# Moving the operand splits around the output projection of a neighbourhood-attention layer, and one more up product ahead of the second half

## The chip, the cores and the metric

The kernel runs on one core of one Trainium2 chip. The metric is the device time of one execution in microseconds; the time given for a kernel is the median of several runs.

## The reference

One trunk of two layers over 1024 latent tokens (a grid 64 wide) and 256 context tokens, width 1024. Layer 0 mixes with grouped-query attention and a bidirectional recurrence; layer 1, which the change touches, mixes with 2-D neighbourhood attention over 16 heads of 64 channels, then projects the heads' outputs with `w_out` (1024 x 1024). Both layers end with a gated feed-forward net of 2816 channels with a width-3 convolution. Cut to layer 1:

```python
h = rms_norm(x, norm_pre_mix) * (1 + sc1) + sh1
y = neighbourhood_attention(h, h_ctx) @ odd_w_out            # (1024, 1024)
x = x + g1 * rms_norm(y, norm_post_mix)
h = rms_norm(x, norm_pre_ffn) * (1 + sc2) + sh2
a, g = split(conv3(h @ w_up) + b)
x = x + g2 * rms_norm((silu(g) * a) @ w_down, norm_post_ffn)
```

## The kernel before

Every product is done at nearly float32 accuracy on TensorE by splitting each operand into a rounded part and a remainder and adding three products: rounded x rounded, rounded x remainder, remainder x rounded. A **split** is two instructions: ScalarE (ACT) writes the rounded part with a cast, then another engine subtracts it from the raw tile to get the remainder. In `w_split` the raw tile is a piece of `w_out` (`w_raw`, 128x512, two buffers), the parts are `w_hi` and `w_lo`; in `o_split` it is a 128-channel chunk of the attention's output (`o_raw`, one buffer; read back from the scratch `ocd`), the parts are `o_h` and `o_l`. Remainders of both are subtracted on VectorE (DVE).

**Attention** (`odd_attention`) runs 128 jobs, one for each of 8 tiles of 128 queries of 16 heads. The Python loop makes one pass per job, called a *turn* here, and six more passes that finish the last jobs (the *drain*). The order in which the passes write instructions is the order on PE, ACT, DVE and POOL (`in_order`). A turn holds: the scores `c_s` of job i (PE); their maximum, the *reduce*, with the bias (DVE, `c_p<-c_s`); the exponential of job i-1 (ACT); the transposes `c_pt` of job i-3 (PE) and the split of what they give (`c_ph` on ACT, `c_pl` on DVE); half of the value products `c_pv` of an earlier pair (PE); the reciprocal `rl` of job i-1 (DVE) and the *divide* by it (POOL, `c_p<-c_p,rl`); every second turn `finish` (ACT `c_o`, DVE), whose results go to `ocd`, or for the last two heads to the tile `oL`.

Between these, `step(n)` draws n pieces from the generator `fill`. It first gives the projections of q and k, and when they are used up, shortly before turn 112, it gives `odd_out_ahead`: the splits of `w_out`'s first half (columns 0 to 511), of the chunks of `o`, the first k-steps of the output projection (`out_step`, tiles 0 and 1, columns 0 to 511, three matmuls each) and then the splits of `w_out`'s second half, in the order they are written there, some 2.5 pieces in a turn, so that they lie between other instructions of a turn.

**Output projection and norm** (`odd_out_norm`): after the drain, `steps()` writes 114 k-steps (three matmuls each) into four PSUM banks, and between them the work on finished tiles (square, root, scaling, residual: `square`, `post`, `add`, `squares`, `scale`). The tile's bank is used again by a later tile, so a k-step can wait for `post` (DVE, `y<-g_ps`). The second half of the tokens needs its own `o_split` of each chunk, read from `ocd` again; they are written at steps 2, 4, ... 16.

**Feed-forward front** (`second_front`): first products of the up projection run before the second half of the tokens is normalised. `first(j)` is a product of the weight quarter `A11` of channel block j, `first_out(j)` copies its result out of PSUM (`f_p`), and a second product with the quarter `A12` adds to the same bank. `second_half` then transposes the second half of the tokens (`n_pc`, `n_pt`, `n_pv`), and splits the sums that a Strassen-like scheme needs. `split` here leaves its remainder to GpSimd (POOL).

Of the kernel before, what the change touches and what calls it, by code (L numbers as in the profile page):

```python
# [11 lines left out]
F32 = mybir.dt.float32  # L12
# [3 lines left out]
OP = mybir.AluOpType  # L16
# [4 lines left out]
P = 128  # L21
# [44 lines left out]
class Trunk:  # L66
# [1227 lines left out]
    def odd_out_norm(self, xs, first_half, op, load, early):  # L1294
# [66 lines left out]
        def steps():  # L1361
            seq = [(0, 0, KT - 1), (1, 0, KT - 1)]
            seq += [(i, 1, k) for i in range(2) for k in range(KT)]
            seq += [(i, h, k) for i in range(2, 8) for h in range(2) for k in range(KT)]
            chains, waits, groups = [], [], list(range(KT))
            for n, (i, h, k) in enumerate(seq):
                if (i, h) not in ps:
                    ps[i, h] = self.banks2[2 * h + i if i < 2 else 2 * (i % 2) + h]
                self.out_step(i, h, k, ps[i, h])
                for f in waits:  # L1370
                    f()
                waits = []
                for c in list(chains):
                    if next(c, "end") == "end":
                        chains.remove(c)
                if k == KT - 1:
                    if h == 0:
                        ms1[i] = self.small.tile([P, 2], F32, name="y_ms")
                        waits.append(lambda i=i: square(ps[i, 0], ms1[i], 0))
                    elif i < 7:  # L1380
                        chains.append(chain(i))
                if n % 2 == 0 and 2 <= n < 2 + 2 * KT:
                    c = (n - 2) // 2
                    self.o_split(raws[c] if c < KT - 1 else self.oL, c, 1)
# [12 lines left out]
            for c in chains:  # L1397
                for _ in c:
                    pass
# [21 lines left out]
    def ffn_up(self, l, src, ctx, x_src, x_dst, hp, pp, tp, es, beside):  # L1421
# [123 lines left out]
        def second_front():  # L1545
# [24 lines left out]
            pp, tp = (self.pool(es, n, 1, space=PSUM) for n in ("u_psum", "t_psum"))  # L1570
            first(0)
            first_out(0, self.wp.tile([P, 512], F32, name="f_p1", tag="w_A21h", bufs=1))
            next(tail)
            product(st["G", 0][:, :512], ("A12",), "B21", False, True)
            split(1, "A11")
            first(1)
            for _ in tail:
                pass
            nx.close()
            sp, cw = up_pool()  # L1580
            total(0, "S1", "A21", OP.add, "A22")
# [7 lines left out]
            next(sums)  # L1589
            return sp, cw, sums  # L1590

        X, sp = {}, None
        with self.in_order(*self.compute, behind=l == 1), ExitStack() as loads:
            sp, cw, sums = second_front() if l == 1 else up_front()

# [1 line left out]
            for j in range(FK):  # L1597
# [8 lines left out]
                if j:  # L1606
                    gate_start(j - 1)
                    split(j, "S4")
                if j or l == 0:
                    product(st["G", j][:, :512], ("A12",), "B21", False, True)  # L1610
                if j:
                    gate_end(j - 1)
# [550 lines left out]
    def odd_attention(self, gp, tp, pp, sp):  # L2163
# [197 lines left out]
        at = {"job": 0}  # L2361
        fill = project()

        def step(n):
            for _ in range(n):
                next(fill, None)

        jobs = [(h, b, ql) for h in range(CH) for b in (0, 3, 1, 2) for ql in range(2)]
        with self.in_order(*self.compute):
# [52 lines left out]
    def odd_out_ahead(self, at):  # L2422


        nc, a = self.nc, self.a
        W, O, raws = self.oW, self.oX, {}
        halves = [(k, h) for h in range(2) for k in range(KT)]

        def w_load(m):
# [5 lines left out]
        def w_split(m):  # L2435
# [3 lines left out]
            hi, lo = (w[:, 512 * h:512 * h + 512] for w in W[k])  # L2439
            raw = raws.pop(m)  # L2440
            nc.scalar.copy(hi, raw)
            nc.vector.tensor_tensor(out=lo, in0=raw, in1=hi.bitcast(F32), op=OP.subtract)
            w_load(m + 2)

        def o_load(c):
# [2 lines left out]

        w_load(0)
        w_load(1)  # L2450
        for m in range(2):
            w_split(m)
            yield
        while at["job"] < 112:
            yield
        o_load(0)
        w_split(2)
        yield
        for k in range(6):
            if k + 3 < KT:  # L2460
                w_split(k + 3)
                yield
            self.o_split(raws["o"], k, 0)
            if k < 5:
                o_load(k + 1)
            yield
            for i in range(2):
                self.out_step(i, 0, k, self.banks2[i])
                yield
        for m in range(KT, 2 * KT):  # L2470
            w_split(m)
            if m == KT + 3:
                o_load(6)
            yield
        self.o_split(raws["o"], 6, 0)
        yield
        for i in range(2):
            self.out_step(i, 0, 6, self.banks2[i])
            yield

    def o_split(self, raw, k, half):

# [210 lines left out]
```

## Time and profile before

| | us |
|---|---|
| median of 3 runs (3399.95 to 3403.27) | 3402.81 |
| profiled execution, whole | 3395.78 |
| its span | 3393.9 |
| layer 1, last turns and drain (2535 to 2608 of the span) | 73 |
| output projection and norm (2608.5 to 2698.1) | 89.6 |
| feed-forward front and block 0 (2698 to 2757) | 59 |

Times in the profile are microseconds from the span's start. A timeline row gives start, duration, engine, source line, operation and, in brackets, how long the engine was idle before it and what ended that. A windows row gives, for a stretch, its length, then busy time and number of instructions of PE, PEld (weight load), DVE, ACT and POOL, the granted TensorE clock (1.00 is full), the busy share of the DMA engines and GB/s.

### The profile page before, as it was taken

How to read it: one execution, taken by the hardware profiler on the slowest of the kernel's cores; microseconds unless marked ns; L12 is line 12 of the kernel's file. 1: busy time of each engine (PE TensorE's matmuls, PEld its weight loads, DVE VectorE, ACT ScalarE, POOL GpSimd, SP SyncE). 2: the span in 40 equal slices, each digit the busy share in tenths (PEclk: the TensorE clock that was granted, in tenths of full speed). 3: DMA queues.
4: the chain of work that ended last, by engine and by line, in shares of the span. 5: the costliest groups of instructions: out<-in, count | busy, mean ns of one | idle time of the engine just before them, and what ended most of it. 6: DMA issues, size and time to landing. Idle time of an engine off the chain costs nothing.

```text
span 3393.9 us, 48741 instructions
## 1 busy us (share of the span) xinstructions
PE 3117.6 (92%) x18364; PEld 2565.9 (76%) x18364; DVE 2038.5 (60%) x3421; ACT 1485.7 (44%) x2643; POOL 1528.8 (45%) x1155
## 2 busy tenths in 40 slices
PE   5899998869999599999999989999997989999997
PEld 2776776658887488888878768889986758888785
DVE  3625666647775754454577773377776465555778
ACT  3223222256664543333434353466665443433443
POOL 1310111187775466666620011577763367777201
PEclk8999999969999699999999989999999989999998
DMA  7524333321111221111275773222224212222856
GB/s 235 161 94 137 126 122 119 102 89 38 51 44 55 104 73 69 67 69 68 73 269 182 273 247 124 75 67 62 65 71 145 101 63 81 85 84 76 279 184 211
DMA packets 201100, 393.48 MB, mean 116 GB/s; under 512 B 23184, under 2 KB 84624, under 8 KB 200864
## 3 DMA queue, kind: packets, MB, share of 16 engines
q1 hardware_dynamic: 191680, 358.38, 32.2%
q0 software_dynamic: 9184, 31.99, 2.5%
q8 instruction: 144, 2.36, 0.3%
q14 instruction: 92, 0.75, 0.1%
HBM read 316.86 MB, written 73.81 MB: 115 GB/s over the span
## 4 chain that ended last, share of the span: by engine, by line
PE 76%; DVE 10%; DMA 4%; ACT 4%; issue 3%; POOL 2%; SPq 1%; POOLq 0%; ACTq 0%; DVEq 0%
PE g_ps L119 21%; PE u_g L119 13%; PE d_ps L119 11%; PE u_v L119 10%; PE u_pc L119 4%; PE a_pv L119 2%; PE c_pv L119 2%; PE c_s L119 2%; PE a_pt L949 2%; PE c_pt L2325 2%; PE mod_ps L119 1%; DVE a_pl L951 1%; PE a_s L119 1%; PE o_ps L119 1%; ACT a_ph L950 1%
## 5 line engine op out<-in xcount | busy, mean ns | idle before, releaser
L127 POOL TENSOR_TENSOR rs_r<-rs_e,mhalf 128x1 f32<-128x1 f32 (+3 forms) x106 | 81.5, 769 | 965.7 <-DVE rs_e L126 965.6
L119 PE MATMUL d_ps<-d_Bh,d_Ah 128*128 128x512 f32 x704 | 276.8, 393 | 10.6 <-ACT d_Bh L1739 10.3
L2308 POOL TENSOR_SCALAR c_p<-c_p,rl 128x640 f32<-128x640 f32 (+1 forms) x128 | 231.7, 1811 | 111.9 <-DVE rl L2307 86.4
L119 PE MATMUL d_ps<-d_Bl,d_Ah 128*128 128x512 f32 x704 | 277.8, 395 | 3.1 <-DVE d_Bl L1740 2.7
L119 PE MATMUL d_ps<-d_Bh,d_Al 128*128 128x512 f32 x704 | 276.5, 393 | 2.0 <-DVE d_Al L1740 1.9
L929 POOL TENSOR_SCALAR a_p<-a_p,rl 128x1280 f32<-128x1280 f32 (+1 forms) x80 | 240.0, 3002 | 72.4 <-DVE rl L928 60.4
L119 PE MATMUL g_ps<-xh,w_hi 128*128 128x512 f32 (+1 forms) x640 | 257.3, 402 | 7.9 <-ACT w_hi L563 6.5
L119 PE MATMUL g_ps<-xh,w_lo 128*128 128x512 f32 (+1 forms) x640 | 238.2, 372 | 2.6 <-POOL w_lo L2208 1.4
L119 PE MATMUL g_ps<-xl,w_hi 128*128 128x512 f32 (+1 forms) x640 | 238.7, 373 | 0.0
L1461 DVE TENSOR_TENSOR f_u<-u_v,f_p 128x512 f32<-128x512 f32 x88 | 60.5, 688 | 186.1 <-PE u_v L119 186.1
L951 DVE TENSOR_TENSOR a_pl<-a_pt,a_ph 128x512 fp32r<-128x512 f32 (+1 forms) x200 | 118.8, 603 | 85.0 <-ACT a_ph L950 84.9
L119 PEld LDWEIGHTS d_ps<-d_Bh,d_Ah 128*128 128x128 f32 x704 | 133.4, 189 | 40.7 <-ACT d_Bh L1739 11.4
L1447 POOL TENSOR_TENSOR w_S4l<-w_s,w_S4h 128x512 fp32r<-128x512 f32 x44 | 57.1, 1298 | 231.0 <-ACT w_S4h L1446 231.0
L119 PEld LDWEIGHTS d_ps<-d_Bl,d_Ah 128*128 128x128 f32 x704 | 133.2, 189 | 35.3 <-DVE d_Bl L1740 6.2
L119 PEld LDWEIGHTS g_ps<-xh,w_hi 128*128 128x128 f32 x640 | 122.3, 191 | 47.0 <-issue 27.5
L119 PEld LDWEIGHTS d_ps<-d_Bh,d_Al 128*128 128x128 f32 x704 | 133.5, 190 | 30.6 <-DVE d_Al L1740 3.3
L950 ACT CAST a_ph<-a_pt 128x512 fp32r<-128x512 f32 (+1 forms) x200 | 102.8, 518 | 121.0 <-PE a_pt L949 120.9
L2328 DVE TENSOR_TENSOR c_pl<-c_pt,c_ph 128x256 fp32r<-128x256 f32 (+1 forms) x256 | 113.7, 470 | 53.4 <-ACT c_ph L2327 52.2
L119 PE MATMUL g_ps<-w_hi,xh 128*128 128x512 f32 (+1 forms) x368 | 142.4, 387 | 2.8 <-ACT w_hi L498 1.6
L2327 ACT CAST c_ph<-c_pt 128x256 fp32r<-128x256 f32 (+1 forms) x256 | 99.0, 414 | 99.2 <-PE c_pt L2325 97.2
L119 PEld LDWEIGHTS g_ps<-xh,w_lo 128*128 128x128 f32 x640 | 121.7, 190 | 25.5 <-POOL w_lo L2208 1.8
L119 PE MATMUL g_ps<-w_lo,xh 128*128 128x512 f32 (+1 forms) x368 | 137.9, 375 | 2.7 <-DVE w_lo L2069 1.9
(568 smaller groups left out, 9891.4 us busy)
## 6 DMA issues: line engine op xcount, KB each, us to landing
m_raw<-in_w_mod SPq DMA_DIRECT2D x96, 512.0 KB
w_raw<-in_w_up SPq DMA_DIRECT2D x88, 512.0 KB
d_rawA<-actd SPq DMA_DIRECT2D x77, 512.0 KB
d_rawB<-in_w_down SPq DMA_DIRECT2D x74, 512.0 KB
actd<-f_t SPq DMA_DIRECT2D x22, 640.0 KB
d_t<-in_w_down SPq DMA_DIRECT2D x22, 512.0 KB
actd<-f_t SPq DMA_DIRECT2D x22, 512.0 KB
d_s<-actd SPq DMA_DIRECT2D x20, 512.0 KB
```

The source lines that it names most:

```text
L119: return self.nc.tensor.matmul(out, lhsT, rhs, start=start, stop=stop, skip_group_check=True, **k)
L127: nc.gpsimd.tensor_tensor(out=r[:p, :n], in0=e[:p, :n], in1=self.mhalf[:p, :n], op=OP.pow)
L929: nc.gpsimd.tensor_scalar(Pt[:, :nk], Pt[:, :nk], rl, None, op0=OP.mult)
L949: nc.tensor.transpose(pt[:, m, qt * P:(qt + 1) * P], Pt[:, kts[j + m] * P:(kts[j + m] + 1) * P], self.ident)
L950: nc.scalar.copy(ph[:, j:j + n], pt[:, :n])
L951: nc.vector.tensor_tensor(out=pl[:, j:j + n], in0=pt[:, :n], in1=ph[:, j:j + n].bitcast(F32), op=OP.subtract)
L1447: nc.gpsimd.tensor_tensor(out=lo, in0=part(j, name), in1=hi.bitcast(F32), op=OP.subtract)
L1461: nc.vector.tensor_tensor(out=out, in0=x, in1=y, op=OP.add)
L2308: nc.gpsimd.tensor_scalar(Pt[:, :n], Pt[:, :n], rl, None, op0=OP.mult)
L2325: nc.tensor.transpose(pt[:, j, :], Pt[:, (src + j) * P:(src + j + 1) * P], self.ident)
L2327: nc.scalar.copy(vap(ph, o, dims), pt[:, :cnt])
L2328: nc.vector.tensor_tensor(out=vap(pl, o, dims), in0=pt[:, :cnt], in1=vap(ph, o, dims).bitcast(F32), op=OP.subtract)
```

## The change

Four edits, all in the order of work.

1. `odd_out_ahead` is parted. The splits become a generator of their own, `odd_out_chores`, drawn once at the end of a turn from turn 112 (behind the reciprocal and the `finish`), and twice in a pass of the drain. The first half of `w_out` and the chunks of `o` alternate, one split in a turn; then come the eight splits of `w_out`'s second half.
2. The k-steps stay in `fill`; a step k is written only in a turn that begins after `o_split` k was written (`at["seen"]`).
3. The remainders of `w_out`'s second half are subtracted on GpSimd and not on VectorE. In `odd_out_norm` the splits of the second half's chunks are written at steps 11, 14, ... 32, and with each the load of a later chunk.
4. In `second_front` the `A11` split of block 1 stands earlier, and block 1's `A12` split, its `first_out` and its `A12` product are done there, ahead of the second half. They are left out of blocks 0 and 1 of the loop.

```diff
@@ odd_out_norm, steps()
-                if n % 2 == 0 and 2 <= n < 2 + 2 * KT:
-                    c = (n - 2) // 2
+                if n % 3 == 2 and 11 <= n < 11 + 3 * KT:
+                    c = (n - 11) // 3
                     self.o_split(raws[c] if c < KT - 1 else self.oL, c, 1)
                     load_o(c + 3)
@@ second_front
             first_out(0, self.wp.tile([P, 512], F32, name="f_p1", tag="w_A21h", bufs=1))
+            split(1, "A11")
             next(tail)
             product(st["G", 0][:, :512], ("A12",), "B21", False, True)
-            split(1, "A11")
             first(1)
             for _ in tail:
                 pass
+            split(1, "A12")
+            p1 = st["p1"]
+            first_out(1, self.wp.tile([P, 512], F32, name="f_p1", tag="w_A21l", bufs=1))
+            ahead["p1"], st["p1"] = st["p1"], p1
+            product(st["G", 1][:, :512], ("A12",), "B21", False, True)
             nx.close()
@@ ffn_up, loop over blocks j
-                if j or l == 0:
+                if j > 1 or l == 0:
                     product(st["G", j][:, :512], ("A12",), "B21", False, True)
...
-                if not ctx:
+                if not ctx and j:
                     split(n, "A12")
...
-                first_out(n)
+                if "p1" in ahead:
+                    st["p1"] = ahead.pop("p1")
+                else:
+                    first_out(n)
@@ odd_attention
             for i in range(N + 6):
-                at["job"] = i
+                at["seen"] = at["ready"]
...
                 step(1)
+                if i >= N - 16:
+                    next(chores, None)
+                if i >= N:
+                    next(chores, None)
+            for _ in chores:
+                pass
+            at["seen"] = KT
@@ odd_out_chores (was the first part of odd_out_ahead)
-            nc.vector.tensor_tensor(out=lo, in0=raw, in1=hi.bitcast(F32), op=OP.subtract)
+            (nc.gpsimd if h else nc.vector).tensor_tensor(out=lo, in0=raw, in1=hi.bitcast(F32), op=OP.subtract)
             w_load(m + 2)
...
+        o_load(0)
+        m = 0
+        for k in range(KT - 1):
+            w_split(k)
+            yield
+            self.o_split(raws["o"], k, 0)
+            if k < KT - 2:
+                o_load(k + 1)
+            at["ready"] = k + 1
+            yield
+        w_split(KT - 1)
+        yield
+        for m in range(KT, 2 * KT):
             w_split(m)
             yield
+    def odd_out_ahead(self, at):
+        for k in range(KT - 1):
+            while at["seen"] <= k:
                 yield
             for i in range(2):
                 self.out_step(i, 0, k, self.banks2[i])
                 yield
```

**DVE, turns 122 to 124** (the row with 128x512 scores is turn 123; ISA is the reduce). Before:

```order
L2356 TENSOR_TENSOR oL<-c_pv,c_o 64x256
L2442 TENSOR_TENSOR w_lo<-w_raw,w_hi 128x512
L2296 ISA c_p,nm<-c_s,c_be_19058 128x512
L2296 ISA nm 128x1
L2442 TENSOR_TENSOR w_lo<-w_raw,w_hi 128x512
L2328 TENSOR_TENSOR c_pl<-c_pt,c_ph 128x2x128
L2442 TENSOR_TENSOR w_lo<-w_raw,w_hi 128x512
L2328 TENSOR_TENSOR c_pl<-c_pt,c_ph 128x2x128
L2307 RECIPROCAL rl<-l 128x1
L2442 TENSOR_TENSOR w_lo<-w_raw,w_hi 128x512
```

The same turns after the change:

```order
L2364 TENSOR_TENSOR oL<-c_pv,c_o 64x256
L2457 TENSOR_TENSOR w_lo<-w_raw,w_hi 128x512
L2304 ISA c_p,nm<-c_s,c_be_19058 128x512
L2304 ISA nm 128x1
L2336 TENSOR_TENSOR c_pl<-c_pt,c_ph 128x2x128 x2
L2315 RECIPROCAL rl<-l 128x1
L2507 TENSOR_TENSOR o_l<-o_raw,o_h 128x512
```

Three remainders around one reduce have become one in a turn, always the last instruction of it.

**ACT, the end of the drain and the first steps of the norm** (`junk` is a square). Before:

```order
L2327 CAST c_ph<-c_pt 128x3x128
L2327 CAST c_ph<-c_pt 128x2x128
L2352 COPY c_o<-c_pv 64x256 x2
L2496 CAST o_h<-oL 128x512
L1325 ACTIVATE junk,y_ms<-g_ps_19056 128x512
L1325 ACTIVATE junk,y_ms<-g_ps_19057 128x512
L2496 CAST o_h<-w_raw 128x512 x2
L2496 CAST o_h_25189<-w_raw 128x512 x2
L1325 ACTIVATE junk,y_ms<-o_ps_25185 128x512
```

After:

```order
L2456 CAST w_hi<-w_raw 128x512 x2
L2335 CAST c_ph<-c_pt 128x3x128
L2335 CAST c_ph<-c_pt 128x2x128
L2360 COPY c_o<-c_pv 64x256
L2456 CAST w_hi<-w_raw 128x512 x3
L2360 COPY c_o<-c_pv 64x256
L2506 CAST o_h<-oL 128x512
L1325 ACTIVATE junk,y_ms<-g_ps_19056 128x512
L1325 ACTIVATE junk,y_ms<-g_ps_19057 128x512
L1325 ACTIVATE junk,y_ms<-o_ps_25185 128x512
L2506 CAST o_h<-w_raw 128x512
```

Casts of the second half of `w_out` now stand among the drain's last casts, and the square of `o_ps` stands ahead of the casts of the second half's chunks and no longer behind four of them.

**ACT, the feed-forward front.** Before:

```order
L1483 COPY f_p_25916<-u_g 128x512
L1325 ACTIVATE junk,y_ms<-a_x 128x512 x2
L1446 CAST w_A11h<-w_raw 128x512
L1344 ACTIVATE y<-a_x,rs_r 128x512
L1249 ACTIVATE x_t_25972<-n_pc,mod_3_5200,mod_4_6137 128x512
```

After:

```order
L1483 COPY f_p_25916<-u_g 128x512
L1446 CAST w_A11h<-w_raw 128x512
L1325 ACTIVATE junk,y_ms<-a_x 128x512 x2
L1344 ACTIVATE y<-a_x,rs_r 128x512
L1446 CAST w_A12h<-w_raw 128x512
L1483 COPY f_p_25966<-u_g 128x512
L1249 ACTIVATE x_t_25990<-n_pc,mod_3_5200,mod_4_6137 128x512
```

The cast of `A12` and a second copy out of PSUM now stand between the scaling of the last tile and the first transposed tile of the second half.

More of the change, by code (lines that the diff above doesn't have):

```diff
@@ L1590, in second_front @@
             return sp, cw, sums
-        X, sp = {}, None
+        X, sp, ahead = {}, None, {}
         with self.in_order(*self.compute, behind=l == 1), ExitStack() as loads:
@@ L2359, in finish @@
             nc.sync.dma_start(self.ocd[h // 2][r:r + 64, 256 * b:256 * b + 256], o)
-        at = {"job": 0}
-        fill = project()
+        at = {"ready": 0, "seen": 0}
+        fill, chores = project(), self.odd_out_chores(at)
         def step(n):
@@ L2420, in odd_attention, with odd_out_chores @@
         self.oL = at["oL"]
-    def odd_out_ahead(self, at):
+    def odd_out_chores(self, at):
         nc, a = self.nc, self.a
-        W, O, raws = self.oW, self.oX, {}
+        W, raws = self.oW, {}
         halves = [(k, h) for h in range(2) for k in range(KT)]
@@ L2450, in odd_out_ahead @@
         w_load(1)
-        for m in range(2):
+        o_load(0)
[11 more added lines that the diff above has]
+        for m in range(KT, 2 * KT):
             w_split(m)
             yield
[L2454 to L2461, printed above, removed]
+    def odd_out_ahead(self, at):
+        for k in range(KT - 1):
+            while at["seen"] <= k:
                 yield
[L2463 to L2466, printed above, removed]
             for i in range(2):
@@ L2469, in odd_out_ahead @@
                 yield
[L2470 to L2479, printed above, removed]
     def o_split(self, raw, k, half):
```

## The prediction

> **What bounds the kernel now.** I read the page first (busy time, chain), then busy time by stretch around the places that the change touches, then the timelines of those places.
>
> ```profile
> PE 3117.6 (92%) x18364; PEld 2565.9 (76%) x18364; DVE 2038.5 (60%) x3421; ACT 1485.7 (44%) x2643; POOL 1528.8 (45%) x1155
> PE 76%; DVE 10%; DMA 4%; ACT 4%; issue 3%; POOL 2%; SPq 1%; POOLq 0%; ACTq 0%; DVEq 0%
> ```
>
> ```profile
> 2480.00:2520.00 40.00, 40.00 (x271) 36.29 (x271) 29.21 (x78) 26.78 (x65) 29.67 (x21) 1.00 0.20 51
> 2535.00:2560.00 25.00, 19.96 (x109) 17.08 (x109) 18.66 (x47) 15.14 (x37) 11.06 (x6) 0.86 0.53 162
> 2580.00:2600.00 20.00, 13.08 (x72) 10.94 (x72) 13.25 (x34) 12.57 (x30) 8.21 (x5) 0.83 0.18 53
> 2705.00:2730.00 25.00, 17.26 (x71) 10.41 (x69) 20.20 (x21) 13.89 (x23) 15.24 (x12) 0.93 0.16 46
> 2730.00:2760.00 30.00, 21.06 (x57) 13.62 (x58) 21.27 (x24) 13.85 (x21) 12.37 (x9) 0.66 0.11 35
> ```
>
> As a whole PE bounds the kernel. Where the change lies it does not: up to 2520 PE is full, in the last turns it is idle for 20 to 35% with the clock down to 0.83, and in the feed-forward front DVE is the busiest. So time counts in the order DVE, ACT, POOL there, and a PE saving counts only where PE is what others wait for.
>
> **Part 1: the last turns.** The first row is the reduce of turn 112, the last that of turn 127, 15 turns later (the last reduce of the kernel); between them stand two of turns 115 and 120, and then the DVE groups of that stretch.
>
> ```profile
> 2536.49 0.67 DVE L2296 CUSTOM_DVE_ANT_0 c_p<-c_s,c_be 128x512 f32<-128x512 f32 x1
> 2550.62 0.68 DVE L2296 CUSTOM_DVE_ANT_0 c_p<-c_s,c_be 128x512 f32<-128x512 f32 x1
> 2568.23 0.69 DVE L2296 CUSTOM_DVE_ANT_0 c_p<-c_s,c_be 128x512 f32<-128x512 f32 x1 [0.77 <-PE c_s L119]
> 2597.12 0.82 DVE L2296 CUSTOM_DVE_ANT_0 c_p<-c_s,c_bi 128x640 f32<-128x640 f32 x1
> ```
>
> ```profile
> L2328 DVE TENSOR_TENSOR c_pl<-c_pt,c_ph 128x256 fp32r<-128x256 f32 (+1 forms) x40 | 17.8, 472 | 9.2 <-ACT c_ph L2327 9.2
> L2442 DVE TENSOR_TENSOR w_lo<-w_raw,w_hi 128x512 fp32r<-128x512 f32 x14 | 10.6, 760 | 4.5 <-ACT w_hi L2441 4.4
> L2296 DVE CUSTOM_DVE_ANT_0 c_p<-c_s,c_bi 128x640 f32<-128x640 f32 x12 | 9.8, 818 | 4.1 <-PE c_s L119 4.1
> L2497 DVE TENSOR_TENSOR o_l<-o_raw,o_h 128x512 fp32r<-128x512 f32 x7 | 5.5, 791 | 1.1 <-ACT o_h L2496 1.1
> L2356 DVE TENSOR_TENSOR oL<-c_pv,c_o 64x256 f32<-64x256 f32 x8 | 3.3, 417 | 2.3 <-ACT c_o L2352 2.1
> L2307 DVE RECIPROCAL rl<-l 128x1 f32<-128x1 f32 x18 | 2.8, 154 | 0.0
> L2296 DVE DVE_READ_ACCUMULATOR2_ANT nm<- 128x1 f32 x16 | 1.3, 81 | 0.0
> ```
>
> 15 turns take 60.6 us, 4.04 each. In the new order a turn has one split behind all else. Its DVE work: reduce 0.82 and read 0.08, two `c_pl` 0.94, reciprocal 0.15, half a `finish` 0.21, one remainder 0.77: 2.97 us. ACT and POOL were busy for less than DVE in both stretches above. The reloads get two turns each and so hide, as long as an `o_raw` needs no more than about 4.3 us:
>
> ```profile
> 2561.41 4.28 DMA o_raw<-ocd
> ```
>
> Of the waits for `c_ph` (9.2 us in 16 turns) I leave less than half, 0.23 a turn, since a k-step still stands ahead of every second turn's transposes and waits for the last `o_l`: 3.2 us a turn. Bounds: 2.9 with no wait left; 3.5, the pace from turn 115 to 120 before (17.6 us for five, with more than one split a turn). 15 x (3.2 - 4.04) = **-12.6 us** (-17 to -8). Ahead of turn 112, two remainders leave the turns 110 and 111:
>
> ```profile
> 2533.29 1.06 DVE L2442 TENSOR_TENSOR w_lo<-w_raw,w_hi 128x512 fp32r<-128x512 f32 x1
> ```
>
> The first held the reduce behind it by about 1.0: **-1.0** (-1.5 to 0).
>
> **Part 2: the drain.** The eight second-half splits, which lay among turns 121 to 126, now start in turn 127. Their remainders are POOL instructions queued with the last two divides, and each reload waits for the remainder two before it (two buffers). ACT's casts wait for these loads with `c_ph` and `c_o` of the last jobs queued behind them.
>
> ```profile
> 2599.01 3.89 POOL L2308 TENSOR_SCALAR c_p<-c_p,rl 128x640 f32<-128x640 f32 x2 [0.30 <-ACT c_p L2302]
> 2704.27 1.28 POOL L1447 TENSOR_TENSOR w_A11l<-w_raw,w_A11h 128x512 fp32r<-128x512 f32 x1 [0.58 <-ACT w_A11h L1446]
> 2585.57 2.59 DMA w_raw<-in_odd_w_out
> 2588.18 0.62 ACT L2441 CAST w_hi<-w_raw 128x512 fp32r<-128x512 f32 x1 [0.33 <-DMA w_raw<-in_odd_w_out]
> 2607.95 0.62 ACT L2496 CAST o_h<-oL 128x512 fp32r<-128x512 f32 x1 [0.48 <-DVE oL L2356]
> ```
>
> From the start of turn 127's reduce: reciprocal done at 1.9; divide 1.9 (3.89 for two); remainder 1.3 (the same shape on POOL); divide 1.9; remainder 1.3: split 9 is done at 8.3. Then splits 11 and 13, each load 2.6 + cast 0.6 + remainder 1.3 and hand-overs 0.15 = 4.65: 17.6. Load 15: 20.2; cast 0.6, the last `c_o` 0.4, `finish` 0.4, hand-overs: `o_h<-oL` starts at 21.7. Before it started at 2607.95 - 2597.12 = 10.8. **+10.9 us** (+9 with the four remainders of this chain at DVE's 0.77; +16 with its three loads at the 4.28 of `o_raw`).
>
> PE stands idle for about the last 6 us of this. What a gap costs beyond itself shows in part 3's rows: 7.5 us lost after a wait of 3.95, with the clock at 0.75, and of those PE waited 4.6:
>
> ```profile
> PE g_ps L119 <- DVE y L1330: 4.6, 2, 3.9
> ```
>
> The other 2.9 is the slow clock, and I take as much for this gap: **+2.9** (0 to +3.5). The Trainium skill ("TensorE: Matmul & The Clock Gate", Part 1) has it that one idle window of about 3.4 us halves the clock until about one busy window has passed: by that the price would be an estimated 1.7, and the sum 1.2 lower.
>
> **Part 3: the norm.** PE's longest wait there:
>
> ```profile
> 2614.85 0.62 ACT L2496 CAST o_h<-w_raw 128x512 fp32r<-128x512 f32 x1 [3.50 <-DMA w_raw<-ocd]
> 2619.70 0.62 ACT L2496 CAST o_h<-w_raw 128x512 fp32r<-128x512 f32 x1 [1.73 <-DMA w_raw<-ocd]
> 2625.40 0.80 PE L119 MATMUL g_ps<-w_hi,o_h 128*128 128x512 f32 x1 [3.95 <-DVE y L1330]
> 2621.10:2634.60 13.50, 8.92 (x27) 0.75 0.42 158
> 2636.00:2649.50 13.50, 13.50 (x61) 1.00 0.42 145
> ```
>
> ACT waits for four loads from `ocd` with the square of tile 0 queued behind, so `post` frees the bank late. In the new order the square comes first and the first split at step 11, 7.5 us after the norm starts. On SP its load stands behind the last `w_raw` load (out at 17.6 in part 2's count, before the norm starts), four `a_x` and the gate, as before, when it landed 6.3 us after the start (2614.85 against 2608.5): it is there. Over these 13.5 us 34 matmuls fewer ran than in the full stretch after, 34 x 0.22 = **-7.5 us** (-8 to -4). What is late next: nothing down to step 26, since `post` follows its square within 3 us and the bank is wanted 5.5 us after.
>
> **Part 4: the feed-forward front.**
>
> ```profile
> 2701.78 0.50 PE L119 MATMUL u_g<-x_B210h,w_A12h 128*128 128x512 f32 x1 [0.72 <-ACT f_p L1483]
> 2706.10 0.72 ACT L1344 ACTIVATE y<-a_x,rs_r 128x512 f32<-128x512 f32 x1 [1.92 <-POOL rs_r L127]
> 2708.01 0.60 PE L1248 MATMUL n_pc<-ident,y 128*128 128x128 f32 x4
> 2732.36 0.68 DVE L1279 TENSOR_TENSOR x_t<-x_t,x_t 128x512 f32<-128x512 f32 x1
> 2736.31 6.78 DVE L1284 TENSOR_TENSOR x_t<-x_t,x_t 128x512 f32<-128x512 f32 x4
> 2736.27 1.27 POOL L1447 TENSOR_TENSOR w_A12l<-w_raw,w_A12h 128x512 fp32r<-128x512 f32 x1 [4.38 <-ACT w_A12h L1446]
> 2765.05 0.50 PE L119 MATMUL u_v<-x_T30h,w_S3h 128*128 128x512 f32 x1 [2.04 <-DVE f_u L1461]
> ```
>
> The second half starts with `n_pc` at 2708.0, and from there the stage is a chain of ACT and DVE. The moved product stands ahead of `n_pc`. The `A11` cast now comes early, so `first(1)` follows without a wait and ends 24 matmuls of 0.23 after 2701.78, at 2707.3; then the copy and its hand-over (0.72, and the pipeline's end) 0.9, then twelve matmuls 2.7: `n_pc` at 2710.9, **+2.9**. `A12`'s remainder on POOL leaves the stretch at 2736, where four DVE sums take 1.70 each beside POOL work against 0.68 alone; one such collision goes: **-1.0**. The product taken out of block 1 (2.7 us of PE) I cost at nothing: block 1's third product waits for `f_u`, the end of a DVE chain that does not use it; the wait of 2.04 grows. If that cover fails, it is worth -2.7. Together **+1.9** (-1 to +3).
>
> **The sum**, against the profiled execution (3395.78; 1.9 of it outside the span): -1.0 - 12.6 + 10.9 + 2.9 - 7.5 + 1.9 = -5.4, so 3390.4. The median of the runs stands 7.0 higher (3402.81); I put the forecast there: **3397.4 us**. What this kernel's measurement can tell from no change is about 0.2%, 6.8 us. The forecast's own range is -11 to -1.
>
> **The rivals.**
>
> *The turns reach the engine bound.* All `c_ph` waits go, 2.9 us a turn: 15 x 0.3 = 4.5 more, -9.9, 3392.9. For it: the last turns before, with no split in them, take 2597.12 - 2595.07 = 2.05 us. Against it: the k-step's wait for `o_l`.
>
> ```profile
> 2595.07 0.82 DVE L2296 CUSTOM_DVE_ANT_0 c_p<-c_s,c_bi 128x640 f32<-128x640 f32 x1 [1.68 <-PE c_s L119]
> ```
>
> *The splits are not hidden.* `o_raw` has one buffer; where its load takes the 4.28 above plus a queue delay, each turn pair waits, and the pace stays 3.5: -8.1 for -12.6, sum -0.9, 3401.9. For it: the loads that ACT waited for before; against: they had 1.6 turns, now two.
>
> *The remainder is held by the divide* (slower). Behind the reciprocal, each remainder starts just as POOL starts the divide. Were it held to that divide's end, it would cost 1.88 - 0.28 at the offset of this row from the remainder at 2533.29, of which 0.38 (1.06 against the 0.68 of the same shape in part 4) is paid there already: 1.2 a turn, 15 x 1.2 = +18, sum +12.6, 3415.4. It decides from 0.81 us a turn, (5.4 + 6.8)/15.
>
> ```profile
> 2533.01 1.88 POOL L2308 TENSOR_SCALAR c_p<-c_p,rl 128x640 f32<-128x640 f32 x1 [1.02 <-ACT w_hi L2441]
> ```
>
> For it speaks the 1.70 against 0.68 of part 4; against it, that this remainder was done at 2534.35, with the divide running to 2534.89. The Trainium skill ("SBUF — State Buffer", Who interferes with whom) says that a DVE instruction with two SBUF inputs and a GpSimd one that reads SBUF exclude each other, the later fully blocked; by that rule it would go this way, and the row disagrees.
>
> **How the numbers follow.** Forecast 50% (a little under half of its range lies beyond -6.8), engine bound 22%, not hidden 18%, held by the divide 10%. Faster by over 0.2%: 0.22 + 0.20 = 0.42. Slower: 0.10. Within: 0.48. The range goes from -15 (engine bound, the drain at +9, no slow clock) to +4 (not hidden, and the drain at +16): 3388 to 3407; it leaves out most of the last rival and the far end of the first.
>
> **What would show it.** Reduce 112 to 127 in about 48 us with remainders below 1.1; the last reduce to `o_h<-oL` about 21.7, with ACT waiting for `w_raw`; half clock as the norm starts, then no PE wait for `y`; `n_pc` 12.8 us after the norm's end (2698.1), where it was 9.9; and a longer wait for `f_u`. I am wrong if the drain does not grow, if the turns keep 4 us, or if block 1 gets shorter.

## The result

| | before | after |
|---|---|---|
| median of 7 runs, us | 3400.16 (3397.45 to 3403.27) | 3389.68 (3387.37 to 3393.15) |
| profiled execution | 3395.78 | 3389.68 |
| its span | 3393.9 | 3387.9 |

The ratio is 0.9969, with a 95% interval of 0.9958 to 0.9981: 10.5 us faster (6.5 to 14.3). That is 0.31%, beyond the 0.2% that was held to be told from no change, though the interval begins at 0.19%. The median lies inside the predicted range of 3388 to 3407, 1.7 us from its lower end and 7.7 us under the 3397.4 forecast. The prediction had given "within 0.2%" the largest chance, 0.48; faster, which came, had 0.42.

For the kernel as a whole the page after says what it said before: PE carries the chain.

```profile
PE 3120.6 (92%) x18364; PEld 2565.9 (76%) x18364; DVE 2030.9 (60%) x3413; ACT 1485.6 (44%) x2643; POOL 1540.8 (45%) x1163
PE 76%; DVE 10%; ACT 4%; DMA 4%; issue 3%; POOL 2%; SPq 0%; POOLq 0%; ACTq 0%; DVEq 0%
```

The change shows by stretch. First two windows rows of before, turns 112 to 127 and the drain, then the same two of after with the 13.5 us of the norm in which PE had waited for `post`:

```profile
2536.50:2597.10 60.60, 45.55 (x259) 37.62 (x257) 43.50 (x105) 38.07 (x89) 30.01 (x18) 0.90 0.41 127
2597.10:2608.60 11.50, 6.68 (x52) 5.84 (x50) 5.70 (x16) 5.73 (x15) 5.38 (x3) 1.00 0.18 55
```

```profile
2536.40:2582.10 45.70, 40.83 (x263) 34.34 (x264) 39.42 (x98) 34.72 (x84) 31.87 (x18) 1.00 0.42 133
2582.20:2604.20 22.00, 8.89 (x47) 7.33 (x45) 5.63 (x16) 9.99 (x22) 14.41 (x11) 0.62 0.39 120
2621.10:2634.60 13.50, 13.21 (x59) 10.62 (x58) 8.94 (x20) 7.32 (x18) 2.78 (x5) 1.00 0.67 226
```

In the turns PE goes from 75% busy at clock 0.90 to 89% at 1.00. The drain doubles and PE is busy for 40% of it. The norm's hole is filled: 59 matmuls where there were 27.

These are the timeline rows after that answer to those of the prediction: the reduces of turns 112 and 127, two remainders in the turns, the drain's casts and two of its remainders on POOL, the start of the norm, its one wait for `y`, and the front.

```profile
2536.39 0.69 DVE L2304 CUSTOM_DVE_ANT_0 c_p<-c_s,c_be 128x512 f32<-128x512 f32 x1
2577.86 0.80 DVE L2507 TENSOR_TENSOR o_l<-o_raw,o_h 128x512 fp32r<-128x512 f32 x1 [0.73 <-ACT o_h L2506]
2580.88 1.89 POOL L2316 TENSOR_SCALAR c_p<-c_p,rl 128x640 f32<-128x640 f32 x1 [1.68 <-DVE rl L2315]
2581.19 1.03 DVE L2457 TENSOR_TENSOR w_lo<-w_raw,w_hi 128x512 fp32r<-128x512 f32 x1
2582.14 0.81 DVE L2304 CUSTOM_DVE_ANT_0 c_p<-c_s,c_bi 128x640 f32<-128x640 f32 x1
2588.99 1.27 POOL L2457 TENSOR_TENSOR w_lo<-w_raw,w_hi 128x512 fp32r<-128x512 f32 x1
2589.90 0.62 ACT L2456 CAST w_hi<-w_raw 128x512 fp32r<-128x512 f32 x1 [4.13 <-DMA w_raw<-in_odd_w_out]
2597.49 0.62 ACT L2456 CAST w_hi<-w_raw 128x512 fp32r<-128x512 f32 x1 [1.39 <-DMA w_raw<-in_odd_w_out]
2598.19 1.28 POOL L2457 TENSOR_TENSOR w_lo<-w_raw,w_hi 128x512 fp32r<-128x512 f32 x1 [1.78 <-ACT w_hi L2456]
2602.06 0.62 ACT L2456 CAST w_hi<-w_raw 128x512 fp32r<-128x512 f32 x1 [2.23 <-DMA w_raw<-in_odd_w_out]
2603.55 0.62 ACT L2506 CAST o_h<-oL 128x512 fp32r<-128x512 f32 x1 [0.48 <-DVE oL L2364]
2604.22 0.80 PE L119 MATMUL g_ps<-w_hi,o_h 128*128 128x512 f32 x1 [4.54 <-ACT o_h L2506]
2624.34 0.50 PE L119 MATMUL g_ps<-w_hi,o_h 128*128 128x512 f32 x1 [0.29 <-DVE y L1330]
2691.81 0.50 PE L119 MATMUL u_g<-x_B210h,w_A12h 128*128 128x512 f32 x1 [0.72 <-ACT f_p L1483]
2701.09 0.60 PE L1248 MATMUL n_pc<-ident,y 128*128 128x128 f32 x4
2729.38 5.72 DVE L1284 TENSOR_TENSOR x_t<-x_t,x_t 128x512 f32<-128x512 f32 x4
2749.37 0.77 PE L119 MATMUL u_v<-x_T20h,w_S2h 128*128 128x512 f32 x1 [3.56 <-DVE f_t L1469]
2757.61 0.50 PE L119 MATMUL u_v<-x_T30h,w_S3h 128*128 128x512 f32 x1
2763.18 0.39 PE L119 MATMUL u_g<-x_B110h,w_A11h 128*128 128x512 f32 x1
```

15 turns take 45.75 us, 3.05 each. The drain takes 21.41, and ACT waits for `w_raw` in it six times, 11.4 us in all (the summed waits from 2582 to 2605):

```profile
ACT w_hi L2456 <- DMA w_raw<-in_odd_w_out: 11.4, 6, 4.1
```

The norm's first 5 us run at a reduced clock:

```profile
2604.22:2609.22 5.00, 5.00 (x14) 3.96 (x15) 0.68 (x1) 1.38 (x4) 0.00 (x0) 0.61 0.99 318
```

`n_pc` comes 12.88 us after the norm's end (2688.21).

These marks divide each kernel's trace into five stretches: the reduce of turn 110 to that of 112; 112 to 127; 127 to `o_h<-oL` (the drain); the first norm matmul to the front's first `A12` matmul (the norm); and from there to block 1's `A11` product (the front). Lengths in us from one profiled execution of each; the last column is the whole way, with the step from `o_h<-oL` to the first matmul (0.7) in it.

| kernel | 110-112 | 112-127 | drain | norm | front | all |
|---|---|---|---|---|---|---|
| before | 7.42 | 60.63 | 10.83 | 93.16 | 68.86 | 241.6 |
| after | 6.01 | 45.75 | 21.41 | 87.59 | 71.37 | 232.8 |
| before + norm's edit | 7.42 | 62.32 | 10.83 | 87.31 | 69.15 | 237.7 |
| attention's edits alone | 6.37 | 45.78 | 21.19 | 92.50 | 71.04 | 237.6 |
| before + front's edit | 7.45 | 61.07 | 10.83 | 93.47 | 71.47 | 245.0 |
| after, front undone | 6.75 | 45.80 | 21.21 | 88.10 | 69.49 | 232.0 |
| after, DVE remainders | 6.47 | 44.99 | 16.82 | 87.88 | 71.41 | 228.2 |
| after, split mid-turn | 6.42 | 40.61 | 19.40 | 87.09 | 71.20 | 225.4 |
| interleaved | 6.49 | 51.73 | 13.13 | 87.95 | 73.05 | 233.0 |
| interleaved, front undone | 6.00 | 51.38 | 14.14 | 88.13 | 69.47 | 229.8 |
| after, six raw buffers | 6.90 | 45.04 | 14.06 | 88.43 | 73.00 | 228.1 |
| mid-turn + DVE, front undone | 6.48 | 40.46 | 16.30 | 88.52 | 71.01 | 223.4 |
| the same + six buffers | 6.90 | 41.52 | 14.51 | 88.01 | 69.48 | 221.1 |

By this table the change is worth -8.8 us. Stretches resolve it better than whole runs: the reduce of turn 110, ahead of which all these kernels are the same, stands anywhere from 2525.65 to 2535.28 in the thirteen traces. How well they resolve it is seen where kernels share a stretch's order. The turns of the old order take 60.6 to 62.3 in three traces, those of the new order 45.75 to 45.80 in three; the old drain takes 10.83 three times, the new one 21.2 to 21.4.

### The profile page after: what moved, and what is told of

It is laid out like the page before. It is cut to its first block, busy times and chain, and to the rows that moved or that the text cites. A ratio compares the mean times of both kernels' runs of the same rounds, so it can differ in the third digit from the quotient of the medians.

```text
span 3387.9 us, 48743 instructions
## 1 busy us (share of the span) xinstructions
PE 3120.6 (92%) x18364; PEld 2565.9 (76%) x18364; DVE 2030.9 (60%) x3413; ACT 1485.6 (44%) x2643; POOL 1540.8 (45%) x1163
## 4 chain that ended last, share of the span: by engine, by line
PE 76%; DVE 10%; ACT 4%; DMA 4%; issue 3%; POOL 2%; SPq 0%; POOLq 0%; ACTq 0%; DVEq 0%
PE g_ps L119 21%; PE u_g L119 13%; PE d_ps L119 10%; PE u_v L119 10%; PE u_pc L119 4%; PE a_pv L119 2%; PE c_pv L119 2%; PE c_s L119 2%; PE a_pt L949 2%; PE c_pt L2333 2%; DVE a_pl L951 1%; PE mod_ps L119 1%; PE a_s L119 1%; PE o_ps L119 1%; DMA m_raw<-in_w_mod 1%
## 5 line engine op out<-in xcount | busy, mean ns | idle before, releaser
L929 POOL TENSOR_SCALAR a_p<-a_p,rl 128x1280 f32<-128x1280 f32 (+1 forms) x80 | 240.3, 3007 | 71.4 <-DVE rl L928 60.6
L119 PEld LDWEIGHTS d_ps<-d_Bh,d_Ah 128*128 128x128 f32 x704 | 133.9, 190 | 39.0 <-ACT d_Bh L1747 10.2
L119 PE MATMUL g_ps<-w_hi,xl 128*128 128x512 f32 (+1 forms) x368 | 138.4, 376 | 0.6 <-DVE xl L299 0.6
```

The costliest lines, as they stand in the source:

```text
L119: return self.nc.tensor.matmul(out, lhsT, rhs, start=start, stop=stop, skip_group_check=True, **k)
L929: nc.gpsimd.tensor_scalar(Pt[:, :nk], Pt[:, :nk], rl, None, op0=OP.mult)
```

## The experiments

Ratios are to the kernel before, from runs on the same chip.

**One part of the change alone.** The norm's edit on the kernel before:

```diff
-                if n % 2 == 0 and 2 <= n < 2 + 2 * KT:
-                    c = (n - 2) // 2
+                if n % 3 == 2 and 11 <= n < 11 + 3 * KT:
+                    c = (n - 11) // 3
```

> The kernel before with one edit: the second half's chunks are split at steps 11, 14, ... 32 of the norm and not at 2, 4, ... 16. Theory (terms add, each paid at its own place): PE's wait for `post` and the slow clock behind it go, -7.5 us (-8 to -4), ratio about 0.9978, from first norm matmul to `n_pc` about 92 us instead of 99.5; nothing ahead of the norm changes. Rival (the stall belongs to loads that come late whatever the order): the wait moves to a later k-step that needs the second half's chunks, 0 to -3 us, and a wait for `post` or for `o_h` of over 1 us stays in the norm.

Ratio 0.9976 (0.9962 to 0.9990), -8.2 us. The norm is 5.9 us shorter and has one wait for `y`, of 0.29 us; the theory holds. But it also shows what the prediction had not foreseen. The first windows row is the norm's first 5 us in the kernel before:

```profile
2608.62:2613.62 5.00, 5.00 (x21) 3.82 (x22) 0.67 (x1) 1.38 (x4) 0.00 (x0) 1.00 0.95 296
```

these are the same 5 us here:

```profile
2606.89:2611.89 5.00, 5.00 (x15) 3.98 (x16) 0.67 (x1) 1.37 (x4) 0.00 (x0) 0.66 0.87 265
```

and this is the matmul that begins them, in the timeline:

```profile
2606.89 0.80 PE L119 MATMUL g_ps<-w_hi,o_h 128*128 128x512 f32 x1 [1.56 <-ACT o_h L2496]
```

The drain is the same 10.83 us and the wait ahead the same 1.56, yet the norm starts at clock 0.66 and runs 15 matmuls where the kernel before ran 21 at 1.00: 6 x 0.22 = 1.3 us, at 0.22 us for a matmul at full clock. Without it the norm's edit is worth 7.2.

The attention's edits alone are the kernel after, with the norm's condition as in the `-` lines above and the front as before:

> The kernel after with the norm's splits back at steps 2, 4, ... 16 and the front as in the kernel before, so that only the attention's part of the change is left (one split a turn behind the reciprocal, the second half's remainders on POOL). Theory (terms add): turns 112 to 127 at 3.05 us as in the kernel after, -16 with the two turns ahead, the drain +10.6, half clock as the norm starts +2, the norm's wait for `post` stays: -3 to -4 us against the kernel before. Rival (the norm's wait is a matter of when the loads from `ocd` land, and the drain now ends after their issue): the wait for `post` shrinks or goes without the norm's edit, -6 to -9 us. Second rival (a gap ahead and a slow start add to the norm's wait): 0 to +3.

Ratio 0.9974 (0.9964 to 0.9983), -8.8 us; by the stretches -4.0. The two don't agree: the runs' interval, 5.8 to 12.2 us, leaves out the theory's 3 to 4 and takes in the first rival's 6 to 9, while the stretches, from one trace of each kernel, give what the theory said. Turns and drain are those of the kernel after. Of PE's waits in the norm, 4.6 us before, this is left:

```profile
2620.83 0.50 PE L119 MATMUL g_ps<-w_hi,o_h 128*128 128x512 f32 x1 [2.21 <-DVE y L1330]
2629.76 0.50 PE L119 MATMUL g_ps<-w_hi,o_h 128*128 128x512 f32 x1 [1.58 <-DVE y L1330]
```

So the wait shrinks to 3.8 without the norm's edit, a little of the first rival; the norm's edit still took 4.9 us more off (92.50 to 87.59). The front here is 2.2 longer than before although nothing in it changed: 1.6 of that lies in block 1's products from the third on, at a reduced clock.

The front's edit alone, and the kernel after without it (this diff, and `split(1, "A11")` back behind the first `A12` product):

```diff
-            split(1, "A12")
-            p1 = st["p1"]
-            first_out(1, self.wp.tile([P, 512], F32, name="f_p1", tag="w_A21l", bufs=1))
-            ahead["p1"], st["p1"] = st["p1"], p1
-            product(st["G", 1][:, :512], ("A12",), "B21", False, True)
             nx.close()
...
-                if j > 1 or l == 0:
+                if j or l == 0:
```

> The kernel before with the front's edit alone: block 1's `A11` split earlier, its `A12` split, `first_out` and `A12` product ahead of the second half. Theory of the prediction: `n_pc` 2.9 later, one collision of DVE and POOL less, the product taken out of block 1 gives nothing because the DVE chain to `f_u` sets its third product: +1.9 us (norm end to third product of block 1 from 66.9 to 68.8). Rival: the product taken out pays, because the wait moves from one operand to another: -2.7, in all -0.8 or less. Rival on the other side: a longer idle PE in block 1 halves its clock once more, +4.

> The kernel after without the front's edit. Theory (the front costs 1.9, by the trace after about 2.5): 2 to 2.5 us less than the kernel after, -12 to -13 us against the kernel before, about 3387.3; this would be faster than both kernels. Rival (the front's edit pays for itself later, since a turn of the feed-forward loop starts with one product done): 0 to 2 us more than the kernel after.

Ratios 1.0005 (0.9995 to 1.0014), +1.7 us, and 0.9957 (0.9941 to 0.9973). Neither is told from its neighbour by its runs, but the stretch tells: with the edit 71.2 to 71.5 (after, front alone, DVE remainders, mid-turn), without it 68.9 to 69.5 (before, norm alone, front undone, interleaved without front, six buffers without front); kernels with a reduced clock in block 1 left aside (73.0 with the edit, 71.0 without). The edit costs about 2 us. It isn't paid back later either: from this last mark to the end of the span are 623.2 to 624.7 us in the six traces with the edit and 621.8 to 623.9 in the seven without. In the trace of the front alone:

```profile
2711.49 0.60 PE L1248 MATMUL n_pc<-ident,y 128*128 128x128 f32 x4
2759.81 0.47 PE L119 MATMUL u_v<-x_T20h,w_S2h 128*128 128x512 f32 x1 [2.02 <-DVE f_t L1469]
2768.06 0.50 PE L119 MATMUL u_v<-x_T30h,w_S3h 128*128 128x512 f32 x1 [0.91 <-DVE f_u L1461]
```

From `n_pc` to the third product are 56.57 us, where the kernel before took 57.04. Over all thirteen traces it is 56.4 to 56.6 with the edit and 57.0 to 57.7 without. A gain of 0.5 to 1.3 us is about what the DVE collision that went is worth (four sums 5.72 for 6.78), and far from the 2.7 of the product taken out of block 1. So that product bought nothing that can be seen: PE waits for `f_t` a product earlier instead.

**The drain.** The remainders of the second half on DVE again:

```diff
-            (nc.gpsimd if h else nc.vector).tensor_tensor(out=lo, ...
+            nc.vector.tensor_tensor(out=lo, ...
```

> The kernel after with the remainders of the second half of `w_out` on DVE again, as in the kernel before; everything else as after. Theory (the drain is a reload loop of two buffers: load, cast, remainder, load): the first two remainders no longer stand behind divides (2.8 us earlier) and each later round is 0.5 shorter (DVE 0.77 for POOL's 1.27): the last reduce to `o_h<-oL` 17 instead of 21.4, and the kernel 4 us under the kernel after (the prediction's own bound for this was 1.9). Rival (the loop is set by the loads, not by the engine of the remainder): 20 to 21, no change. Rival on the other side (`c_pl` and `oL` of the last jobs queue behind the remainders on DVE): 22 or more, slower by 1.

The drain is 16.82 us; the theory said 17. The ratio, 0.9965 (0.9954 to 0.9976), is not told from that of the kernel after.

Six raw buffers instead of two:

```diff
-                raws[m] = self.wp.tile([P, 512], F32, name="w_raw", bufs=2)
+                raws[m] = self.wp.tile([P, 512], F32, name="w_raw", tag=("w_hi", "w_lo")[m % 2], bufs=3)
...
-            w_load(m + 2)
+            for x in range(2):
+                if at["w"] < m + 7:
+                    w_load(at["w"])
+                    at["w"] += 1
```

> The kernel after with six raw buffers for the pieces of `w_out` instead of two (the tiles `w_hi` and `w_lo` of the projection, three of each, which are free by turn 112), and each piece loaded up to six ahead; order of all other work and POOL's remainders as after. Theory (the drain is a reload loop): ACT's waits for `w_raw` (4.1, 1.7, 0.9, 1.4, 1.1 and 2.2 us in the kernel after) go, and `c_ph`, `c_o` and `o_h<-oL` no longer queue behind them: last reduce to `o_h<-oL` 11 to 13 instead of 21.4, -9 us against the kernel after. Rival (POOL's eight remainders and two divides, 14 us of work, hold the drain): 17 or more, -4. Rival on the other side (loads that run ahead delay those of `o_raw`, so the turns slow down): turns 112 to 127 at 48 or more.

Ratio 0.9950 (0.9935 to 0.9965). The drain is 14.06, the turns 45.04. So the reload loop was the cause of 7 of the 10.6 us, and the other 3 are not waits for loads. PE's longest sum of waits, in us, times and longest, from 2578.5 to 2599 (the drain starts at 2583.69):

```profile
PE c_pt L2333 <- POOL c_p L2316: 3.4, 3, 1.6
```

No wait for `w_raw` is left. PE waits for the divides, which stand among the remainders on POOL; POOL is busy all through the last 10 us of the drain. So the first rival has the right engine, but its 17 us did not come.

The second half's splits in the turns instead of the drain:

```diff
-        halves = [(k, h) for h in range(2) for k in range(KT)]
+        halves = [(k, h) for k in range(KT) for h in range(2)]
...
-            w_split(k)
+            w_split(2 * k)
             yield
             self.o_split(raws["o"], k, 0)
+            w_split(2 * k + 1)
```

> The kernel after with the second half's splits of `w_out` moved from the drain into the turns: in a turn with an `o_split` ACT also casts a second-half piece and POOL subtracts it, behind the divide; one `w_raw` load a turn, still two buffers. Theory (drain and slow start of the norm come from these splits alone): last reduce to `o_h<-oL` 11 instead of 21.4, no half clock at the norm's start (-2), and the turns 0.1 longer each because POOL has room (1.9 of 3.05 us used): -9 to -11 us against the kernel after, about 3380. Rival (POOL becomes the bound of every second turn at 1.89 + 1.27 = 3.16, and with hand-overs the pace goes to 3.5): +7 -12 = -5. Rival on the other side (POOL's remainder and DVE's `o_l` hold each other up and the reload stalls ACT ahead of the next exponential): pace 3.9, no gain.

> The one before this in the list (second-half splits in the turns) without the front's edit. Theory: the parts add, and the front's edit costs 1.9: about 2 us less than the one with it, -11 to -13 against the kernel after. Rival (the front's edit pays later): 0 to 1 us more than the one with it.

Ratios 0.9973 (0.9963 to 0.9983) and 0.9967 (0.9954 to 0.9980). The drain fell by 8.3 us, but the turns rose by 6.0, to 3.45 each: the first rival's pace, and not its reason. In the turns ACT waited for loads (the summed waits, 2539 to 2590):

```profile
ACT w_hi L2456 <- DMA w_raw<-in_odd_w_out: 4.7, 4, 2.7
ACT o_h L2505 <- DMA o_raw<-ocd: 3.7, 2, 2.8
```

The divides' group in the same stretch:

```profile
L2316 POOL TENSOR_SCALAR c_p<-c_p,rl 128x640 f32<-128x640 f32 (+1 forms) x16 | 29.9, 1873 | 10.9 <-PE c_s L119 4.7 <-DVE rl L2315 1.9 <-DMA w_raw<-in_odd_w_out 1.5
```

POOL sat idle for 10.9 us ahead of its divides, so it was no bound. In the kernel after ACT waited 1.4 us for loads in the turns, for `o_raw` alone. So the likely cause is one `w_raw` load a turn and an `o_raw` every second one through two and one buffers, which is what the rival on the other side said; this order with more buffers was not tried. By the stretches nothing was gained, 233.0 for 232.8, where the theory had 9 to 11, and the norm still started at a reduced clock (12 matmuls in its first 5 us), where the theory had none. Without the front's edit it is 3.2 us less, 1.6 of which is the reduced clock of block 1 in the first of the two.

**The place in the turn.** The same one split a turn, ahead of the transposes and no longer behind the reciprocal:

```diff
                 step(1)
+                if i >= N - 16:
+                    next(chores, None)
                 if 0 <= i - 3 < N:
                     transposes(*jobs[i - 3], tiles[i - 3][0], 0)
...
-                if i >= N - 16:
-                    next(chores, None)
```

> The kernel after with the one split of a turn moved from its end to just ahead of the transposes, so that ACT's cast stands ahead of `c_ph` and the remainder ahead of `c_pl`; the number of splits in a turn is unchanged. Theory A (the count counts: one split a turn leaves 2.97 us of DVE work a turn, wherever it stands): turns 112 to 127 within 1.5 us of the 45.75 of the kernel after. Theory B (the place counts: work that the next products wait for must not stand behind a load): 3.5 us a turn, 52 or more, 7 us slower than after. The collision of the remainder with the divide behind the reciprocal goes in both (`w_lo` 0.77 instead of 0.95 to 1.05).

Neither theory: 40.61 us, 2.71 a turn, 5.1 us under the kernel after. The place counts, the other way round from theory B. Ratio 0.9957 (0.9942 to 0.9971). Two DVE groups of the turns, the kernel after (2536 to 2577):

```profile
L2336 DVE TENSOR_TENSOR c_pl<-c_pt,c_ph 128x256 fp32r<-128x256 f32 (+1 forms) x29 | 12.4, 466 | 4.3 <-ACT c_ph L2335 4.3
L2457 DVE TENSOR_TENSOR w_lo<-w_raw,w_hi 128x512 fp32r<-128x512 f32 x7 | 6.8, 976 | 0.3
```

and the kernel mid-turn:

```profile
L2336 DVE TENSOR_TENSOR c_pl<-c_pt,c_ph 128x256 fp32r<-128x256 f32 (+1 forms) x30 | 12.7, 462 | 0.0
L2457 DVE TENSOR_TENSOR w_lo<-w_raw,w_hi 128x512 fp32r<-128x512 f32 x8 | 6.8, 849 | 0.0
```

From the view of the tile `o_l`, who waited for it (us, times), after and mid-turn:

```profile
  PEld g_ps L119: 3.6, 7
```

```profile
  PEld g_ps L119: 0.9, 2
```

The windows row of the turns, mid-turn:

```profile
2535.70:2576.30 40.60, 39.84 (x261) 35.18 (x259) 37.68 (x99) 34.48 (x84) 28.97 (x18) 0.97 0.49 149
```

With the split at the turn's end `o_l` comes just ahead of the next turn, whose k-step stands on PE in front of the transposes; the weight loads of the k-steps waited 3.6 us for it, then `c_pl` 4.3 us for `c_ph`. Moved ahead, `o_l` is done in time, both waits nearly go, and PE is busy for 98%, so the turns are bound by PE again.

**Together.** The diffs above put together: split mid-turn, DVE remainders, front undone; and the same with six buffers:

> The three edits that gained by themselves, put together on the kernel after: the split of a turn ahead of the transposes, the second half's remainders on DVE, no front's edit. Theory (terms add): turns 112 to 127 at 40.6, the drain 19.4 less the 4.6 that DVE's remainders gained, about 15, the front -1.9: 11 us under the kernel after, profiled span about 3375. Rival (the drain's gain was the same one that the earlier split already took): drain 19, -7.

> The one before this in the list with the six raw buffers as well. Theory: turns 112 to 127 at 40 to 41, the drain 11 to 12 since no cast waits for a load, no gap ahead of the norm over 1.6 us: 15 us under the kernel after, profiled span about 3371, the best of all. Rival (DVE becomes the bound of the drain with eight remainders of 0.77 among the last `c_pl`): drain 15, no gain over the one without the buffers.

Ratios 0.9931 (0.9914 to 0.9948) and 0.9920 (0.9905 to 0.9934): medians 3376.74 and 3374.71 us. Both beat both kernels; the last is 27 us under the kernel before. The two are not told apart by their runs. Turns and drain of the first are 40.46 and 16.30 (expected 40.6 and 15). With the buffers the drain is 14.51 and not 11 to 12: the rival's length, but DVE is not the engine that PE waits for most. POOL's last two divides, among DVE's remainders, in the timeline of the kernel with the buffers:

```profile
2580.51 4.84 POOL L2311 TENSOR_SCALAR c_p<-c_p,rl 128x640 f32<-128x640 f32 x2 [0.90 <-PE c_pt L2328]
```

and PE's longest sum of waits from 2578.5 to 2599:

```profile
PE c_pt L2328 <- POOL c_p L2311: 3.7, 3, 2.0
```

Two divides took 4.84 us, where two took 3.89 before. What a drain with the divides undisturbed would take was not tried.

## Why the prediction was right, and where it was off

- **The turns, -12.6: measured -14.9.** The rate came near, 3.05 us a turn for 3.2, and the signs that were named came: remainders under 1.1 us, `o_raw` late only twice. The account behind the rate was wrong in part. Its 9.2 us of waits for `c_ph` was read from 2536 to 2608, with the drain in it. In turns 112 to 127 alone it was 6.3, and 4.8 were left. The summed waits of these turns, two rows of before and the same two of after:

```profile
DVE c_pl L2328 <- ACT c_ph L2327: 6.3, 9, 1.3
PE g_ps L119 <- ACT o_h L2496: 7.5, 6, 1.9
DVE c_pl L2336 <- ACT c_ph L2335: 4.8, 8, 0.8
PE g_ps L119 <- ACT o_h L2506: 1.0, 2, 0.7
```

  So it was mostly other waits that went: DVE's for the scores `c_s` (4.8 us) and for `w_hi` (4.4), and the k-steps' wait for `o_h` on PE, which the prediction does not name. In all PE's idle time fell by 10.2 us. Its busy time fell by 4.7 (45.55 to 40.83) as the clock rose from 0.90 to 1.00, a term that the sum lacks. Which edit brought which share is open: no run changed the number of splits alone, or the place of the k-steps alone.

  The rate's two terms erred in opposite ways, and that is luck. The 2.97 of DVE work added mean durations; the window shows 39.42 us busy, 2.63 a turn, where the same rows' durations add up to 43.9, since neighbours overlap. DVE's idle time was 0.42 a turn and not 0.23. So the bound of 2.9, held to be the engine's, was none: the same splits mid-turn ran at 2.71, against PE. The time lies midway between the forecast and the rival of the engine bound (-17.1), whose mechanism did not come, since waits for `c_ph` were left. The two turns ahead gave -1.4 for -1.0, though -0.7 and -1.05 in the two other traces with the same order.
- **The drain, +10.9: measured +10.6.** The chain of waits was as worked out: counted from the last reduce, split 9 was done at 8.1 us (8.3 forecast), split 13 at 17.3 (17.6). The experiments with DVE and with six buffers show that most of it was the reload loop. With the remainders on DVE the drain is 4.6 shorter; the prediction's bound for that, 1.9, was too small.
- **The half clock, +2.9: measured 1.5.** 14 matmuls in the norm's first 5 us for 21. The size is nearer the 1.7 estimated from the Trainium skill ("TensorE: Matmul & The Clock Gate", Part 1). What is not shown is that the gap sets it, 4.54 us long here and not 6. The norm's edit alone lost 1.3 behind the old drain and a wait of 1.56, so the old drain has it in one trace of three; behind every other drain it came, in ten traces of ten (11 to 16 matmuls), six of them with the same wait of 1.56. So it goes with the new drains, but its size can't be charged to the wait ahead of the norm.
- **The norm, -7.5: measured -5.6, or -7.1** with the 1.5 of the slow start taken out. Right, and shown by the norm's edit alone (-7.2).
- **The front, +1.9: measured +2.5** (2.6 for the edit alone, 1.9 when it is undone). `n_pc` came 3.05 later (2.9), and the four sums took 5.72 instead of 6.78, of which 0.5 arrived at the third product in this pair of traces. The forecast that `f_u` would be waited for longer was wrong: after, PE waits 3.56 for `f_t` one product earlier, runs at half clock behind it, and reaches `f_u` when it is there. The cover held all the same.
- **The level.** By the stretches the parts come to -8.8, 3.4 beyond the forecast's -5.4. From profile to profile the kernel after is 6.1 us faster, only 0.7 beyond it, because 1.3 us more lie ahead of turn 110 and 1.5 more behind the last mark. The other 7.0 of the 7.7 us is the step from the profiled execution to the median that the forecast added. The kernel after's profile is at its median, and the kernel before came to 3400.16 over seven runs, 4.4 above its profile. That step is a draw among executions, no mechanism; that the forecast's time stayed in its range in spite of it is in part luck.

Of the rivals, the remainder held by the divide did not happen. `w_lo` of 2581.19, begun 0.31 us into a divide of 1.89, was done 0.55 ahead of its end; the Trainium skill's rule ("SBUF — State Buffer", Summary: rules for kernel authors), that the second one to issue is fully blocked until the first finishes, disagrees with that row. What the divide does cost a remainder is in the last section. The splits were hidden at 3.05, so the pace of 3.5 did not come either; it came only where a `w_raw` was loaded in every turn.

## What to carry to other kernels

Place background work by who reads its result next: behind the critical chain's last instruction it looked free, but a product in front of the next turn waited for it; half a turn earlier it cost 5 us less. Before work is moved out of a busy stretch, count the rounds of its reload loop at the new place: with two buffers it set the drain's length, and buffers that were free by then gave back 7 us. For an engine's bound take its busy time from the windows, not a sum of mean durations.

## What had not been expected of the hardware

- The clock behind equal waits differs from trace to trace. Behind 1.56 us ahead of the norm PE ran 21 matmuls in 5 us (before), 15 (norm's edit alone) and, in the last kernel, 12. In the first two the granted clock of the 10 us ahead was 1.00; in the last it was 0.57 already. The last kernel:

```profile
2593.20:2598.20 5.00, 5.00 (x12) 3.89 (x13) 0.67 (x1) 1.38 (x4) 0.00 (x0) 0.50 0.96 288
```

  What sets it is open; no run here was made to tell.
- A DVE remainder beside a POOL divide pays for the start of the divide only. Three pairs, the first from the kernel after, the others mid-turn:

```profile
2544.63 1.89 POOL L2316 TENSOR_SCALAR c_p<-c_p,rl 128x640 f32<-128x640 f32 x1 [1.14 <-DVE rl L2315]
2544.92 1.05 DVE L2457 TENSOR_TENSOR w_lo<-w_raw,w_hi 128x512 fp32r<-128x512 f32 x1
2546.99 1.89 POOL L2316 TENSOR_SCALAR c_p<-c_p,rl 128x640 f32<-128x640 f32 x1 [1.88 <-PE c_pt L2333]
2547.44 0.89 DVE L2457 TENSOR_TENSOR w_lo<-w_raw,w_hi 128x512 fp32r<-128x512 f32 x1
2535.36 1.89 POOL L2316 TENSOR_SCALAR c_p<-c_p,rl 128x640 f32<-128x640 f32 x1 [0.29 <-ACT c_p L2310]
2536.28 0.69 DVE L2457 TENSOR_TENSOR w_lo<-w_raw,w_hi 128x512 fp32r<-128x512 f32 x1
```

  Begun 0.29 and 0.45 us into the divide, the remainder ends 1.34 after the divide's start both times; begun 0.92 into it, it takes the 0.69 that it takes alone. So it looks held until about 0.65 us (1.34 - 0.69, an estimate) into a divide of 1.89. That fits `w_lo`'s 0.98 on average in the turns of the kernel after and its 0.85 mid-turn, where it begins later in the divide.
- The other way round, two divides took 4.84 us with DVE work among them, 3.89 in the kernel before.
